# Ten warm-up matmuls instead of six, and the first MLP's residual keeps its mean until the last sums are added

## The chip, the core and the metric

The kernel runs on one core of a Trainium2 chip. Its time is in microseconds (us) of device time; several runs are taken and the median is compared. Beside the times there is the trace of one profiled execution, in which TensorE (PE, with its weight loads as PEld), VectorE (DVE), ScalarE (ACT), GpSimd (POOL) and the queue of SyncE (SP), which issues nearly all loads, are recorded instruction by instruction.

## The reference

A decoder trunk of two layers over 256 tokens of width 2048, in float32. The first layer mixes by a short gated convolution, the second by multi-head latent attention; behind each mixer stands an MLP of width 8192. Each of the four sub-layers ends in the same residual and normalisation:

```
h = layer_norm(ALPHA * h + mix, ln_g[layer, 0], ln_b[layer, 0])
h = layer_norm(ALPHA * h + sq_relu_mlp(h, mlp_w1[layer], mlp_w2[layer]), ln_g[layer, 1], ln_b[layer, 1])

def layer_norm(x, g, b):
    mu = mean(x, axis=-1)
    var = mean((x - mu) ** 2, axis=-1)
    return (x - mu) * rsqrt(var + LN_EPS) * g + b

def sq_relu_mlp(x, w1, w2):
    return square(relu(x @ w1)) @ w2
```

A layer norm gives the same result whatever is subtracted from all channels of a token beforehand. The kernel uses this to keep its sums of squares small.

## The kernel before

**Numbers and layout.** The float32 weights are split on the core into two parts, hi (a cast on ScalarE) and lo (a subtraction on VectorE), and TensorE multiplies hi and lo by the activations, which are split in the same way. The residual `xres` lies in SBUF as 16 chunks of 128 channels by 256 tokens: channels on the partitions, tokens along the row.

**The opening.** TensorE first runs `WARM` matmuls of a constant tile with itself into a PSUM tile `warm` that nobody reads. Then the first products (`ps_g`) are formed row by row of an array `opening` as its rows arrive: each row gives four matmuls with its hi part (`hifirst`) and four with its lo part (`lofirst`).

**The norms.** A `Norm` object with index 0 to 2 belongs to each of the first three normalisations; the last one is done elsewhere. `prepare(m)` works on chunk m of the residual: it multiplies by ALPHA and subtracts `mu0`. `mu0` is made at chunk 0 by one matmul with the tile `ones`, whose entries are 1/128: the mean over the first 128 channels of each token, copied by ScalarE from PSUM (`mu0p`) to SBUF (`mu`). `count` adds the chunk to the running sums S and Q, `wide` writes its weighted hi and lo parts `xd`, which the next layer's products read.

**The two MLPs.** `mlp(1, ...)` and `mlp(3, ...)` are one function. Its first part forms eight chunks of the hidden layer directly (`ps_w`). The middle part is planned: products of the first weight matrix (`ps_m`), and a Strassen form of part of the second (`sum1` to `sum7`, held in PSUM banks), are entered as operations of a list `Work`, with costs and dependences. A planner (`arrange`) simulates the engines, and `issue` then emits the instructions in the order it found. Ready operations of ScalarE and VectorE are taken by their due time; an operation that nobody waits for is due at the end and fills what is free. `work` receives the steps of the layer's input normalisation (`normals`), the loads and splits of weights, and, where the MLP is followed by another norm (`after`), the 15 `prepare` steps that are left behind chunk 0. `prepare(0)` is emitted ahead of the plan. The second MLP has no `after`, so its plan has no such steps.

**Behind the plan.** The sums of both column halves are combined on VectorE into eight blocks of 128 tokens by 512 channels: tokens on the partitions here. The rest of the second matrix is multiplied by `down` into PSUM tiles `ps_d`, and `put` adds each to its block. In the first MLP, `to_wide` transposes the blocks on TensorE (`turned`), adds them to `xres` with `add`, and counts and widens each chunk (`summed`). The next layer's first products start while the last blocks are still turned. PSUM tiles are given out in turn from two pools of four banks each.

**What sets the order.** Instructions of one engine run in the order in which they were emitted; engines wait for each other by semaphores. Nearly every instruction goes through one helper, so the profile puts nearly all of them on line L71, and they are told apart by the names of their tiles.

Of the kernel before, what the change touches and what calls it, by code (L numbers as in the profile page):

```python
# [10 lines left out]
F32 = mybir.dt.float32  # L11
F32R = mybir.dt.float32r
AF = mybir.ActivationFunctionType
ALU = mybir.AluOpType
AX = mybir.AxisListType

P = 128
W = 256 + 2
T = 256
D = 2048  # L20
NC = D // P
# [6 lines left out]
ALPHA = 4.0 ** 0.25  # L28
# [14 lines left out]
OPENS = T + OPEN * P  # L43
PLAIN = 2
GROUP = 3
WARM = 6
WO_G = 3

COL = 128
# [4 lines left out]
def trunk(ctx: ExitStack, tc: tile.TileContext, opening, xT, vecs, w_in, w_out, w_kv, w_q, w_uk, w_uv,  # L54
# [5 lines left out]
    class Engine:  # L60
# [3 lines left out]
        def __init__(self, engine):  # L64
            self.engine = engine
# [15 lines left out]
    scalar, vector, tensor, sync = (Engine(e) for e in (nc.scalar, nc.vector, nc.tensor, nc.sync))  # L81
    const = ctx.enter_context(tc.tile_pool(name="const", bufs=1))
    act = ctx.enter_context(tc.tile_pool(name="act", bufs=1))
# [3 lines left out]
    small = ctx.enter_context(tc.tile_pool(name="small", bufs=2))  # L87
# [49 lines left out]
    start = [0]  # L137
# [3 lines left out]
    class Banks:  # L141
# [15 lines left out]
        @classmethod  # L157
        def next(cls):
            cls.count += 1
            if cls.only is not None:  # L160
                return cls.only
            return cls.more if cls.more is not None and cls.count % 8 >= 4 else pmm
# [19 lines left out]
    def prepare(i):  # L182

        kind, *src = stream[i]
        if kind == "unit":
            raw = load_raw(i, src[0])
            hi, lo = ready[i] = parts(i)
            split(hi, lo, tiled(raw))
            yield
            return  # L190
        r1, r2 = (load_raw(f"{i}_{j}", v) for j, v in enumerate(src))

        def finished(r, name):
            w = parts(f"{i}_{name}")
            split(*w, tiled(r))
            return [[v.rearrange("p b c -> p (b c)")[:, o:o + BW] for v in w] for o in (0, BW)]

        out = {}
        out["11"], out["22"] = finished(r1, 1)
        yield  # L200
        out["21"], out["12"] = finished(r2, 2)
        ready[i] = out
        yield
# [24 lines left out]
    def psum(name):  # L228
        return Banks.next().tile([P, 512], F32, tag="mm", name=name)
# [38 lines left out]
    def mm_wide(wps, x, k0=0, k1=NC):  # L268

        for k in range(k0, k1):  # L270
            for w, ps in wps:
                hi, lo = (t[:, k % 8, :] for t in w[k // 8])
                tensor.matmul(ps[:, :W], hi, x[k][:, :W], start=k == 0, stop=False)
                tensor.matmul(ps[:, :W], lo, x[k][:, :W], start=False, stop=False)
                tensor.matmul(ps[:, :W], hi, x[k][:, W:], start=False, stop=k == NC - 1)

    def group_of(n):

        return [(take(), psum("ps_g")) for _ in range(n)]
# [26 lines left out]
    def down(x, put, n):  # L306

        ps = [psum("ps_d") for _ in range(2)]
        for j in range(len(x) // 2):
            w, = take(1)  # L310
            for kk in range(2):
                k = 2 * j + kk
                for t in range(2):
                    dot(ps[t], wide_rows(w, kk), held(x[k], t), k == 0, k == len(x) - 1)
        for t in range(2):
            put(n, t, ps[t])
# [30 lines left out]
    ones = const.tile([P, P], F32, name="ones")  # L347
    col = const.tile([P, COL], F32, name="col")
    vector.memset(ones, 1.0 / P)
    warm = psum("warm")  # L350
    for _ in range(WARM):
        tensor.matmul(warm[:, :P], ones, ones, start=True, stop=True)
# [23 lines left out]
    class Norm:  # L376
# [3 lines left out]
        def __init__(self, idx, scale):  # L380
            self.idx, self.scale = idx, scale
            self.S = act.tile([P, T], F32, tag="S", name=f"S{idx}")
            self.Q = act.tile([P, T], F32, tag="Q", name=f"Q{idx}")
            self.mu0 = act.tile([P, T], F32, tag="mu0", name=f"mu0{idx}")
            self.ws = None

        def prepare(self, m):

# [102 lines left out]
    def residual(ps, m):  # L491

        add(ps[:, T:], m)
        add(ps[:, :T], m)

    def add(ps, m):
        d = xres[:, m, :]
        vector.tensor_tensor(d, d, ps[:, :T], ALU.add)

    def summed(ln, pss, add, m0=0):  # L500

        for m, ps in enumerate(pss, m0):
            add(ps, m)
            ln.count(m)
            ln.wide(m)
# [4 lines left out]
    xres = act.tile([P, NC, T], F32, tag="xres", name="xres")  # L510
# [26 lines left out]
    ln = Norm(0, ALPHA)  # L537
    for m in range(NC):
# [3 lines left out]
        for what in "cub":  # L542
            ps = next(pss)
            f = cbuf[:, m % 2, "cub".index(what), :T]
# [226 lines left out]
    def mlp(idx, ln, after, blocks, fast):  # L771
# [14 lines left out]
        def pair():  # L786
            return fast.tile([P, 8 * P], F32, tag="sf", name="sf", bufs=2)
# [18 lines left out]
        for m in range(QC):  # L806
            if m < GROUP:
# [4 lines left out]
                ps = ws[m][1]  # L812
            else:
                ws = [(take(), psum("ps_w"))]
                mm_wide(ws, ln.xd)
                ps = ws[0][1]
            if m % 2 == 0:
                f = pair()
# [25 lines left out]

        layer, sums = idx // 2, Sums(idx)
        Banks.only = Banks.more
        if after is not None:
            after.prepare(0)
        work, freed, ring, place, entries, frees = Work(), {}, {}, {}, [], {}
        spans = {"A": lambda n: 0.82 * n + 110, "V": lambda n: n / 0.96 + 68}  # L850
        known = lambda deps: [d for d in deps if d is not None]
# [1 line left out]
        def add(engine, n, run, *deps, behind=(), early=0):  # L853
            return work.add(engine, spans[engine](n), run, known(deps), behind, early)
# [27 lines left out]
        normals = {}  # L882
        for k in todo:
# [1 line left out]
            x = add("V", 580, run, normals.get(k - 3))  # L885
            x = add("A", 880, run, x)
            normals[k] = add("V", 256, run, x)
        if after is not None:
            for k in range(1, NC):
                add("V", 256, lambda k=k: after.prepare(k), normals.get(k))  # L890

        fs, used, formed, emptied, halved = {}, {}, {}, [None, None], [None]

# [168 lines left out]
        def block(n, t):  # L1062
            return folded[n][t]

        def put(n, t, ps):
            vector.tensor_tensor(block(n, t), block(n, t), ps, ALU.add)

        h = [(one[:, k // 2, k % 2 * T:(k % 2 + 1) * T], two[:, k // 2, k % 2 * T:(k % 2 + 1) * T]) for k in range(QC)]
        blocks(block, put, h)

    def to_wide(block, put, h):

        def turned(n):
            for c in range(2):
                ps = psum("turned")
                for j in range(4):
                    src = block(n, j % 2)[:, (2 * c + j // 2) * P:(2 * c + j // 2 + 1) * P]
                    tensor.transpose(ps[:, j * P:(j + 1) * P], src, id_t)
                summed(ln, [ps[:, j * T:(j + 1) * T] for j in range(2)], add, 4 * n + 2 * c)

        ln.widen("b")
        for n in range(NB):
            down(h, put, n)
            if n:
                turned(n - 1)
        ln.ws = group_of(GROUP)
        mm_wide(ln.ws, ln.xd, 0, NC - 4)
        turned(NB - 1)
        mm_wide(ln.ws, ln.xd, NC - 4)

    before, ln = ln, Norm(1, ALPHA)


    with tc.tile_pool(name="fast1", bufs=1) as fast:
        mlp(1, before, ln, to_wide, fast)


    with tc.tile_pool(name="att", bufs=1) as ap:
# [63 lines left out]
        f = tmp.tile([P, T], F32, tag="fh", name="fpe", bufs=3)  # L1162
# [3 lines left out]
        for m in range(NK):  # L1166
            ps = next(pss)
# [23 lines left out]
        with tc.tile_pool(name="att2", bufs=2) as a2, \  # L1191
# [82 lines left out]
            after = Norm(2, ALPHA)  # L1274
# [73 lines left out]
    with tc.tile_pool(name="fast2", bufs=1) as fast:  # L1348
        mlp(3, after, None, to_out, fast)
# [88 lines left out]
```

## Time and profile before

| | |
|---|---|
| median of three runs | 2000.35 us (1997.7 to 2000.36) |
| the profiled execution | 2000.64 us |
| its span, first to last instruction | 1998.8 us |
| mean granted TensorE clock | 0.998 |
| busy: PE, DVE, ACT | 1981.9, 1763.3, 1392.6 us |
| HBM read | 383.35 MB, 193 GB/s over the span |

A row of the timeline is start, length, engine, line, operation, tiles (written <- read), shape and count, and in brackets the idle time of the engine before it and what ended it. Rows of equal instructions that follow each other are merged, with the length from the first start to the last end. Matmuls are pipelined: the length of one holds its way through the array, and the distance of two starts is what it takes of the engine. A float32 matmul that isn't split shows as two records. A row of the waits says who waited for whom, with the total in us, the number of times and the longest.

### The profile page before, as it was taken

How to read it: one execution, taken by the hardware profiler on the slowest of the kernel's cores; microseconds unless marked ns; L12 is line 12 of the kernel's file. 1: busy time of each engine (PE TensorE's matmuls, PEld its weight loads, DVE VectorE, ACT ScalarE, POOL GpSimd, SP SyncE). 2: the span in 40 equal slices, each digit the busy share in tenths (PEclk: the TensorE clock that was granted, in tenths of full speed). 3: DMA queues.
4: the chain of work that ended last, by engine and by line, in shares of the span. 5: the costliest groups of instructions: out<-in, count | busy, mean ns of one | idle time of the engine just before them, and what ended most of it. 6: DMA issues, size and time to landing. Idle time of an engine off the chain costs nothing.

```text
span 1998.8 us, 29668 instructions
## 1 busy us (share of the span) xinstructions
PE 1981.9 (99%) x11048; PEld 1733.6 (87%) x11048; DVE 1763.3 (88%) x2646; ACT 1392.6 (70%) x2070; POOL 2.3 (0%) x21
## 2 busy tenths in 40 slices
PE   9999999999999999999999999999999999999997
PEld 8888888988888888888889998898888888888886
DVE  7667667699999999999988888878999999999997
ACT  6444445577887888878856655557788888878871
POOL 0000000000000000000000000000000000000000
PEclk9999999999999999999999999999999999999999
DMA  9655555455666666666664543654666666666673
GB/s 337 230 189 187 189 190 188 155 164 185 208 200 208 203 200 201 203 208 205 214 218 156 165 126 115 209 161 156 196 204 198 204 202 208 205 204 203 199 240 119
DMA packets 107857, 387.39 MB, mean 194 GB/s; under 512 B 11968, under 2 KB 12736, under 8 KB 107712
## 3 DMA queue, kind: packets, MB, share of 16 engines
q1 hardware_dynamic: 107568, 385.36, 60.5%
q8 instruction: 86, 1.41, 0.3%
q14 instruction: 59, 0.48, 0.1%
q10 hardware_dynamic: 144, 0.13, 0.0%
HBM read 383.35 MB, written 2.10 MB: 193 GB/s over the span
## 4 chain that ended last, share of the span: by engine, by line
PE 85%; DVE 8%; ACT 3%; issue 2%; DMA 0%; DVEq 0%; ACTq 0%
PE ps_m L71 25%; PE sum L71 21%; PE ps_u L71 20%; PE ps_d L71 4%; PE ps_w L71 4%; PE ps_g L71 4%; DVE lo L71 4%; DVE w L71 2%; ACT hi L71 1%; PE ps_v L71 1%; PE ps_q L71 1%; PE S L71 1%; PE ps_k L71 1%; PE ps_wo L71 1%; ACT sums L71 1%
## 5 line engine op out<-in xcount | busy, mean ns | idle before, releaser
L71 DVE TENSOR_TENSOR lo<-w,hi 128x1024 fp32r<-128x1024 f32 x536 | 640.0, 1222 | 27.2 <-ACT hi L71 24.3
L71 ACT CAST hi<-w 128x1024 fp32r<-128x1024 f32 x536 | 530.8, 1055 | 141.7 <-DVE w L71 131.5
L71 ACT CAST hi<-raw 128x1024 fp32r<-128x1024 f32 x278 | 289.8, 1051 | 248.8 <-PE ps_u L71 154.9
L71 PE MATMUL ps_m<-xhl,hi 128*128 128x512 f32 x1792 | 446.3, 391 | 1.3 <-ACT hi L71 1.3
L71 DVE TENSOR_TENSOR lo<-raw,hi 128x1024 fp32r<-128x1024 f32 x278 | 334.0, 1222 | 112.3 <-ACT hi L71 39.6
L71 PEld LDWEIGHTS ps_m<-xhl,hi 128*128 128x128 f32 x1792 | 328.9, 188 | 65.6 <-ACT hi L71 1.9
L71 PE MATMUL sum<-hi,hc 128*128 128x512 f32 x736 | 277.9, 391 | 0.5 <-ACT sum L71 0.5
L71 PEld LDWEIGHTS ps_m<-xhl,lo 128*128 128x128 f32 x1792 | 244.3, 190 | 18.0 <-DVE lo L71 0.7
L71 PE MATMUL sum<-lo,hc 128*128 128x512 f32 x656 | 256.5, 391 | 0.0
L71 PE MATMUL ps_m<-xhl,lo 128*128 128x256 f32 x1792 | 250.0, 282 | 0.0
L71 PE MATMUL sum<-hi,ha 128*128 128x512 f32 x640 | 246.4, 389 | 0.0
L71 DVE TENSOR_TENSOR w<-w,w 128x512 f32<-128x512 f32 x312 | 214.5, 687 | 0.7
L71 PE MATMUL ps_u<-xhl_a,hi 128*128 128x512 f32 x704 | 168.1, 391 | 0.0
L71 PEld LDWEIGHTS sum<-hi,hc 128*128 128x128 f32 x736 | 138.6, 188 | 27.2 <-ACT sum L71 1.3
L71 PEld LDWEIGHTS ps_u<-xhl_a,hi 128*128 128x128 f32 x704 | 129.4, 188 | 25.1
L71 PEld LDWEIGHTS sum<-hi,ha 128*128 128x128 f32 x640 | 120.2, 188 | 25.9
L71 PEld LDWEIGHTS sum<-lo,hc 128*128 128x128 f32 x656 | 123.6, 188 | 21.5
L71 ACT COPY sums<-sum 128x512 f32<-128x512 f32 x194 | 109.7, 597 | 13.2 <-PE sum L71 12.6
L71 ACT COPY sum<-sums 128x512 f32<-128x512 f32 x174 | 104.3, 611 | 0.8
L71 ACT ACTIVATE sf<-sf 128x512 f32<-128x512 f32 x120 | 76.7, 639 | 26.9 <-DVE sf L71 25.8
L71 PE MATMUL ps_w<-xd,hi 128*128 128x258 f32 x512 | 94.3, 284 | 0.5 <-DVE xres L71 0.5
L71 PEld LDWEIGHTS ps_u<-xhl_a,lo 128*128 128x128 f32 x704 | 90.3, 191 | 3.4
(197 smaller groups left out, 2756.4 us busy)
## 6 DMA issues: line engine op xcount, KB each, us to landing
w<-in_w_dram SPq DMA_DIRECT2D x224, 512.0 KB, 3.9
w<-in_w2f_dram SPq DMA_DIRECT2D x208, 512.0 KB, 4.6
raw<-in_w_in_dram SPq DMA_DIRECT2D x88, 512.0 KB, 4.4
raw<-in_w_dram SPq DMA_DIRECT2D x64, 512.0 KB, 4.4
raw<-in_w_out_dram SPq DMA_DIRECT2D x32, 512.0 KB, 3.9
raw<-in_w_o_dram SPq DMA_DIRECT2D x32, 512.0 KB, 3.8
raw<-in_w2f_dram SPq DMA_DIRECT2D x16, 512.0 KB, 4.5
row<-in_opening_dram SPq DMA_DIRECT2D x15, 384.0 KB, 4.8
```

What stands on the lines that cost most here:

```text
L71: ins = op(*args, **named)
```

## The change

`WARM` goes from 6 to 10. For the first MLP's norm (index 1) the mean is no longer subtracted from the residual: neither `prepare(0)`, which stood ahead of the plan, nor the 15 planned `prepare` steps are issued. Behind the plan, `means` makes the mean over the first 128 channels as a column, one value per token, with the residual's chunk as stationary operand: two matmuls of one column into `mu0c`, and one small VectorE instruction that scales it to `off`. `put` now adds that column together with each `ps_d`, and `scaled` multiplies the residual by ALPHA while it adds the turned block. The other norms keep `prepare`.

```diff
-WARM = 6
+WARM = 10
...
-            self.mu0 = act.tile([P, T], F32, tag="mu0", name=f"mu0{idx}")
+            self.mu0 = act.tile([P, T], F32, tag="mu0", name=f"mu0{idx}") if idx != 1 else None
             self.ws = None
+
+        def means(self):
+
+            ps = psum("mu0c")
+            for t in range(2):
+                tensor.matmul(ps[:, t:t + 1], xres[:, 0, t * P:(t + 1) * P], ones[:, 0:1], start=True, stop=True)
+            self.off = small.tile([P, 2], F32, tag="off", name="off", bufs=1)
+            vector.tensor_scalar(self.off, ps[:, 0:2], -self.scale, None, ALU.mult)
...
+    def scaled(ps, m):
+        d = xres[:, m, :]
+        vector.scalar_tensor_tensor(d, d, ALPHA, ps, ALU.mult, ALU.add)
...
-        if after is not None:
-            after.prepare(0)
         work, freed, ring, place, entries, frees = Work(), {}, {}, {}, [], {}
...
-        if after is not None:
-            for k in range(1, NC):
-                add("V", 256, lambda k=k: after.prepare(k), normals.get(k))
...
         def put(n, t, ps):
-            vector.tensor_tensor(block(n, t), block(n, t), ps, ALU.add)
-
+            if after is None:
+                vector.tensor_tensor(block(n, t), block(n, t), ps, ALU.add)
+            else:
+                vector.scalar_tensor_tensor(block(n, t), ps, after.off[:, t:t + 1], block(n, t), ALU.add, ALU.add)
+
+        if after is not None:
+            after.means()
...
-                summed(ln, [ps[:, j * T:(j + 1) * T] for j in range(2)], add, 4 * n + 2 * c)
+                summed(ln, [ps[:, j * T:(j + 1) * T] for j in range(2)], scaled, 4 * n + 2 * c)
```

The order of the instructions moves at three places. On TensorE, where the first MLP's plan begins (`ps_w` are the last direct products, `sum` the first Strassen product), there stands before:

```order
L71 MATMUL ps_w<-xd_1_2667,lo_3857 128x258
L71 MATMUL ps_w<-xd_1_2667,hi_3856 128x258
L71 MATMUL mu0p<-xres,ones 128x256
L71 MATMUL sum_4183<-hi_1_3926,hc_3523 128x512
L71 MATMUL sum_4183<-lo_1_3927,hc_3523 128x512
```

and now:

```order
L71 MATMUL ps_w<-xd_1_2671,lo_3860 128x258
L71 MATMUL ps_w<-xd_1_2671,hi_3859 128x258
L71 MATMUL sum_4181<-hi_1_3929,hc_3526 128x512
L71 MATMUL sum_4181<-lo_1_3930,hc_3526 128x512
L71 MATMUL sum_4181<-hi_1_3929,hc_3526 128x512
```

The mean's matmul is gone; the products around it keep their order.

On VectorE, early in the same plan (`lo` a weight's low half, `nu` and `xhl` the normalisation of the input, `xres<-xres,mu` the prepare steps), there stands before:

```order
L71 TENSOR_TENSOR lo_0_4245<-w_4187,hi_0_4244 128x1024
L71 SCALAR_TENSOR_TENSOR xres<-xres,mu_3518 128x256 x3
L71 TENSOR_TENSOR xhl_3522<-xres,xhl_3522 128x256
L71 SCALAR_TENSOR_TENSOR xres<-xres,mu_3518 128x256
L71 TENSOR_TENSOR nu<-xres,ab_3734 128x256
L71 TENSOR_TENSOR nu<-nu,ab_3734 128x256
```

and now:

```order
L71 TENSOR_TENSOR lo_0_4243<-w_4185,hi_0_4242 128x1024
L71 TENSOR_TENSOR xhl_3525<-xres,xhl_3525 128x256
L71 TENSOR_TENSOR nu<-xres,ab_3737 128x256
L71 TENSOR_TENSOR nu<-nu,ab_3737 128x256
L71 TENSOR_TENSOR xhl_3525<-xres,xhl_3525 128x256
```

The prepare steps are gone and what stood behind them has moved up. Within the first twenty or so VectorE instructions, and the first fifty of ScalarE, counted from the first hidden chunks behind, other steps change places as well; from there to the end of the plan both engines have the order of the second MLP's plan, which is the same in both programs. TensorE's order within the plan and SyncE's order of loads are those of before.

On TensorE at the end of the plan (`ps_m` its last product, `ps_d` the first of `down`) there now stands:

```order
L71 MATMUL ps_m<-xhl_3525,hi_3_4355 128x512 x8
L71 MATMUL ps_m<-xhl_3525,lo_3_4356 128x256 x8
L71 MATMUL mu0c<-ones,xres 128x1 x2
L71 MATMUL ps_d<-hi_9002,hc_3526 128x512
L71 MATMUL ps_d<-lo_9003,hc_3526 128x512
```

Before, the first `ps_d` followed the last `ps_m` at once. On VectorE the small instruction behind `mu0c` stands between the last hidden chunk and the low halves of the down weights (`raw`):

```order
L71 TENSOR_TENSOR lo_9015<-raw_9012,hi_9014 128x1024
L71 TENSOR_TENSOR lo_9021<-raw_9018,hi_9020 128x1024
L71 TENSOR_TENSOR sf<-ps_m,t 128x256
L71 TENSOR_SCALAR off<-mu0c 128x2
L71 TENSOR_TENSOR xd_0_8995<-vec,xd_0_8995 128x16x2
L71 TENSOR_TENSOR lo_9027<-raw_9024,hi_9026 128x1024
L71 TENSOR_TENSOR lo_9033<-raw_9030,hi_9032 128x1024
```

All other rows there are those of before, one place later. With `mu0c` the turn of the PSUM banks moves by one from here: `mu0c` takes the bank that held `sum6`, the first `ps_d` that of `sum7`, the second that of `sum5`; before, the two `ps_d` had those of `sum6` and `sum7`.

## The prediction

> **What bounds the kernel now.** I read the page first (busy times, then the chain that ended last), then TensorE's own list of waits, then TensorE's timeline in the opening and at both ends of each MLP's plan.
>
> ```profile
> span 1998.8 us, 29668 instructions
> PE 1981.9 (99%) x11048; PEld 1733.6 (87%) x11048; DVE 1763.3 (88%) x2646; ACT 1392.6 (70%) x2070; POOL 2.3 (0%) x21
> PE 85%; DVE 8%; ACT 3%; issue 2%; DMA 0%; DVEq 0%; ACTq 0%
> ```
>
> TensorE is busy for 99% of the span and carries 85% of the chain. A busy share alone doesn't say that it never stands, so I read its waits over the whole span (total in us, times, longest):
>
> ```profile
> PE ps_m L71 <- ACT hi L71: 1.3, 3, 0.9
> PE ps_g L71 <- ACT hifirst L71: 1.2, 1, 1.2
> PE warm L71 <- DVE col L71: 1.0, 1, 1.0
> PE rstat L71 <- DVE csq L71: 0.8, 1, 0.8
> PE ps_w L71 <- DVE xres L71: 0.5, 1, 0.5
> PE sum L71 <- ACT sum L71: 0.5, 2, 0.3
> ```
>
> These six make 5.3 us of 1998.8; the rest of the list is shorter than 0.5 each. VectorE has 88% and yet TensorE hardly waits for it. So work that leaves VectorE or ScalarE is worth at most the part of these waits that it ends, while what leaves TensorE, or lets it run at full pace, counts in full.
>
> The profiled execution took 2000.64 us, 1.84 more than its span; the median of the three runs is 2000.35. I sum against 2000.64. A measurement of this kernel can tell about 0.2%, 4.0 us, from no change.
>
> **Part 1: four more warm-ups.** TensorE in the opening; start, length, tiles, count, idle time before:
>
> ```profile
> 1.05 2.93 PE L71 MATMUL warm<-ones 128*128 128x128 f32 x12 [1.05 <-DVE col L71]
> 5.22 2.04 PE L71 MATMUL ps_g<-xhl_a,hifirst 128*128 128x512 f32 x4 [1.25 <-ACT hifirst L71]
> 7.92 1.61 PE L71 MATMUL ps_g<-xhl_a,hifirst 128*128 128x512 f32 x4
> 9.84 1.09 PE L71 MATMUL ps_g<-xhl_a,hifirst 128*128 128x512 f32 x4
> 11.24 0.86 PE L71 MATMUL ps_g<-xhl_a,hifirst 128*128 128x512 f32 x3
> ```
>
> Each row of the opening array gives TensorE the same eight matmuls. The first takes 7.92 - 5.22 = 2.70 us, the second 1.92, the third 11.24 - 9.84 = 1.40. TensorE thus starts at about half pace and comes to its full one in the course of the second, some 3 to 4 us after 5.22. The six warm-ups (12 passes) with the idle 1.25 us behind them did not spare it this. The slow pace costs 1.30 + 0.52 = 1.82 us.
>
> Ten warm-ups are 20 passes. One takes about 0.23 us (2.93 less a tail of some 0.4, by 11 distances), so eight more take 1.8: the burst ends near 5.6, 0.4 us after the first real matmul could have started, and TensorE works unbroken from 1.05. The 3 to 4 us that it needed after 5.22 are then over at 4 to 5. If the pace doubles there, the last passes go faster, nothing is delayed and all of 1.82 is gained; if it doubles only with the end of the burst, 1.82 - 0.4 = 1.4. I take 1.4, the case in which the passes cost what the row shows. The other end is a loss of 0.4.
>
> The Trainium skill, "TensorE: Matmul & The Clock Gate", section "Part 1: The HAM clock gate", has a rule for this: the array's clock is halved until it was busy throughout one window of about 3.4 us, and these windows run on freely, whatever the kernel does. Half pace for 3 to 4 us agrees with it. By that rule alone the release could come up to two windows after 1.05, an estimate of 7.9, and the gain would lie anywhere between some 0.4 and 1.8.
>
> Is another engine then the opening's bound? Its last row of data, and TensorE where it uses it:
>
> ```profile
> 23.19 0.69 DVE L71 TENSOR_TENSOR lofirst<-row,hifirst 128x512 fp32r<-128x512 f32 x1
> 28.08 0.40 PE L71 MATMUL ps_g<-xhl_a,hifirst 128*128 128x512 f32 x1
> ```
>
> The data are split by 23.9, 4.2 us early, so a start 1.4 us sooner is covered.
>
> **Part 2: the mean leaves the head of the plan.** That place in the first MLP, and the same in the second, which has no mean there:
>
> ```profile
> 412.07 0.59 PE L71 MATMUL mu0p<-xres,ones 128*128 128x256 f32 x2
> 412.31 0.58 PE L71 MATMUL sum<-hi,hc 128*128 128x512 f32 x1
> 412.73 0.40 PE L71 MATMUL sum<-lo,hc 128*128 128x512 f32 x1
> 1357.15 0.39 PE L71 MATMUL sum<-hi,hc 128*128 128x512 f32 x1
> 1357.38 0.40 PE L71 MATMUL sum<-lo,hc 128*128 128x512 f32 x1
> ```
>
> From mu0p's start to the second sum matmul are 0.66 us, where one sum matmul takes 0.23 in the second MLP: 0.43 gained, of which 0.19 is the slow first sum behind it.
>
> **Part 3: 15 prepare steps leave VectorE's plan.** Their row for all three norms (count, total, mean in ns):
>
> ```profile
> L71 DVE SCALAR_TENSOR_TENSOR xres<-xres,mu 128x256 f32<-128x256 f32 x45 | 17.0, 424 | 0.0
> ```
>
> With chunk 0 they are 16 at 0.42 us here, some 7 us; ScalarE loses one copy. The new order from there on is the second MLP's, so the second MLP's trace is a preview. The last matmuls of both plans:
>
> ```profile
> 996.03 1.11 PE L71 MATMUL ps_m<-xhl,lo 128*128 128x256 f32 x8
> 1939.78 1.12 PE L71 MATMUL ps_m<-xhl,lo 128*128 128x256 f32 x8
> ```
>
> From the first sum to there the first MLP takes 996.03 - 412.31 = 583.72 us, the second 1939.78 - 1357.15 = 582.63. Of the 1.09 between them 0.19 are counted in part 2. The other 0.9 is a wait for hi. TensorE's waits within the first plan and, second row, within the second; then the load and the cast on which the first hangs, and the same pair in the second:
>
> ```profile
> PE ps_m L71 <- ACT hi L71: 1.1, 2, 0.9
> PE ps_m L71 <- ACT hi L71: 0.2, 1, 0.2
> 946.74 0.33 SPq L71 DMA_DIRECT2D w<-in_w_dram  x1
> 952.63 1.05 ACT L71 CAST hi<-w 128x1024 fp32r<-128x1024 f32 x1 [1.38 <-DMA w<-in_w_dram]
> 1891.53 0.33 SPq L71 DMA_DIRECT2D w<-in_w_dram  x1
> 1894.04 2.97 ACT L71 CAST hi<-w 128x1024 fp32r<-128x1024 f32 x3
> ```
>
> In the first MLP the cast began 5.9 us after its load was issued and had stood idle 1.38 for it; in the second it is the last of three casts without a gap. So the order leaves a margin, and one late load used it up. SyncE's order is unchanged and nothing in the change makes loads prompt: between 0 and 0.9 gained, I take half, 0.45. The 7 us of VectorE are otherwise worth nothing, for TensorE's matmuls hid them; were that cover gone, they would have shown as waits of TensorE for VectorE's lo, and the list has none.
>
> **Part 4: the mean behind the plan.** mu0c is two matmuls of one column on a full stationary operand, between ps_m and ps_d. Its nearest like is rstat, two of one column as well:
>
> ```profile
> 1082.15 0.60 PE L71 MATMUL rstat<-col,csq 128*128 128x1 f32 x4 [0.75 <-DVE csq L71]
> 1082.62 0.37 PE L71 MATMUL ps_w<-xd,hi 128*128 128x258 f32 x1
> ```
>
> 0.47 us to the next matmul, and that one is slow by 0.1 to 0.2, as the first sum behind mu0p was: 0.47 to 0.66, I take 0.6 lost. It adds waits: mu0c for the bank of sum6, the second ps_d for that of sum5. VectorE's adds that free them, TensorE's arrival, and what stands ahead of the new off:
>
> ```profile
> 987.69 0.70 DVE L71 TENSOR_TENSOR sums<-sums,sum 128x512 f32<-128x512 f32 x1
> 992.84 1.28 DVE L71 TENSOR_TENSOR sums<-sums,sum 128x512 f32<-128x512 f32 x2
> 996.99 0.40 PE L71 MATMUL ps_d<-hi,hc 128*128 128x512 f32 x1
> 997.84 0.42 DVE L71 TENSOR_TENSOR sf<-ps_m,t 128x256 f32<-128x256 f32 x1
> ```
>
> sum6 is free at 988.4, 8.6 us before TensorE comes; sum5 at 994.1, some 3.5 us before the second ps_d would start. VectorE reaches off at 998.3, when mu0c is through, so off waits for nothing; queued behind it are the gain columns and the lo halves for the following ps_d, each later by one instruction of two columns. Hidden, with the 3.5 us as cover.
>
> The last sums become three-operand instructions: put with a column as scalar, scaled with a constant. The plain adds, and the like of put; that of scaled is the prepare step's row, 0.424:
>
> ```profile
> L71 DVE TENSOR_TENSOR sums<-sums,ps_d 128x512 f32<-128x512 f32 x16 | 10.4, 682 | 8.3 <-PE ps_d L71 8.3
> L71 DVE SCALAR_TENSOR_TENSOR u<-sums,mv,gbt 128x512 f32<-128x512 f32 x8 | 5.9, 741 | 0.0
> L71 DVE TENSOR_TENSOR xres<-xres,turned 128x256 f32<-128x256 f32 x16 | 6.1, 416 | 0.9 <-PE turned L71 0.9
> ```
>
> Eight put at 0.06 more, 0.5 us, lie on VectorE under the next block's matmuls; without that cover they would cost 0.5. Of 16 scaled at 0.008 more, two lie in TensorE's wait ps_w <- DVE xres: 0.02 lost.
>
> **The sum.** -1.4 - 0.43 - 0.45 + 0.6 + 0.02 = -1.66 us; 2000.64 - 1.66 = 1998.98, so 1999.0.
>
> **Rivals.** *The pace comes no sooner.* The burst delays the first real matmul by 0.4 us and buys nothing: 2000.64 + 0.4 - 0.43 - 0.45 + 0.62 = 2000.8. For it speaks that six warm-ups bought nothing that the rows show; against it, that the idle 1.25 us go. Chance 0.21. The skill's freely running window, in the section named, would give this case where it stands badly against the kernel's start, and would make it change from run to run.
>
> *All of it at once.* The full 1.82, both waits of the first plan for hi (1.1), the mean: 2000.64 - 1.82 - 1.1 - 0.43 + 0.62 = 1997.9, about the fastest run shown before (1997.7). For it speaks the lighter VectorE, against it that the second MLP still waits. Chance 0.17. To be faster by over 0.2% the time must fall below 1996.35, which takes 1.5 us that I can't name; but the runs shown differ by 2.7, so I give that 0.07 of the 0.17.
>
> *TensorE stands at the borrowed banks* (slower). If VectorE is late at the end of the plan, mu0c and the second ps_d wait, and off holds the lo halves behind it. It decides where VectorE is more than 3.5 us later than here; each further us costs one. Above 2004.35 (slower by over 0.2%) it takes some 5.4 us more than that; at 9 us it would give 1999.0 + 5.5 = 2004.5. The late load of part 3 held a cast up by 1.4. Chance 0.04.
>
> **The numbers.** The forecast has 0.58; its own range is 1998.1 (1.82 and 0.9 instead of 1.4 and 0.45) to 1999.9 (a gain of 1.0 and no prompt load). The range that holds 8 in 10 takes in the first rival and the second with a little of the runs' spread: 1996.8 to 2001.1. Faster by over 0.2%: 0.09, the 0.07 and a little of the forecast; slower: 0.06, the third rival and 0.02 for what I overlook; within 0.2%: 0.85.
>
> **What would show it.** Right: the first two rows of ps_g less than 1.6 us apart, the first near 5.5; the first sum at once behind ps_w; 582.6 us from it to the last ps_m; ps_d 0.5 to 0.7 us later than at once. Wrong: first rows still 2.7 and 1.9 us apart; a gap ahead of mu0c or the second ps_d; more than 1 us of waits for hi or lo in the first plan.

## The result, and the profile after

The changed kernel takes 2002.46 us (median of 22 runs, 2001.75 to 2003.03), the kernel before, run beside it, 1999.72 (median of 22, 1997.69 to 2001.81). The ratio is 1.0013, with a 95% interval of 1.0007 to 1.0018. So it is slower, by some 2.7 us, less than the 0.2% that the prediction set as its bound; the forecast was 1.7 us faster, and its range ended at 2001.1. The profiled execution took 2003.01 us, 2.37 more than the one of before.

Span, busy times and shares of the chain in the page of the changed kernel:

```profile
span 2001.2 us, 29669 instructions
PE 1986.2 (99%) x11058; PEld 1733.7 (87%) x11058; DVE 1758.8 (88%) x2630; ACT 1392.3 (70%) x2069; POOL 2.3 (0%) x21
PE 94%; DVE 3%; issue 1%; ACT 1%; DMA 1%; SPq 0%; DVEq 0%; ACTq 0%
```

TensorE's share of the chain has grown from 85% to 94%, its busy time by 4.3 us, while its longest wait for `hi` is gone (TensorE's waits, after):

```profile
PE ps_g L71 <- ACT hifirst L71: 0.8, 1, 0.8
...
PE ps_m L71 <- ACT hi L71: 0.3, 2, 0.2
```

So the engine doesn't stand more; it works longer. TensorE's timeline of the changed kernel, at the places that the prediction named, says where:

```profile
411.19 0.39 PE L71 MATMUL sum<-hi,hc 128*128 128x512 f32 x1
411.43 0.40 PE L71 MATMUL sum<-lo,hc 128*128 128x512 f32 x1
...
996.33 1.12 PE L71 MATMUL ps_m<-xhl,lo 128*128 128x256 f32 x8
997.28 0.50 PE L71 MATMUL mu0c<-ones,xres 128*128 128x1 f32 x4
997.65 0.47 PE L71 MATMUL ps_d<-hi,hc 128*128 128x512 f32 x1
997.96 0.39 PE L71 MATMUL ps_d<-lo,hc 128*128 128x512 f32 x1
...
1357.55 0.39 PE L71 MATMUL sum<-hi,hc 128*128 128x512 f32 x1
...
1942.15 1.11 PE L71 MATMUL ps_m<-xhl,lo 128*128 128x256 f32 x8
```

At the first sum it is 1.12 us ahead of before (412.31), as was hoped. Then the first plan takes 996.33 - 411.19 = 585.14 us instead of 583.72, and the lead is gone at the first `ps_d` (0.66 behind). The second plan, in which the change touches no instruction, takes 1942.15 - 1357.55 = 584.60 instead of 582.63. That is 1.97 us, with no wait to show for it. The grouped rows name the matmuls; of before, then of after (count, total us, mean ns):

```profile
L71 PE MATMUL sum<-t,hc 128*128 128x512 f32 x216 | 65.8, 389 | 0.0
L71 PE MATMUL sum<-t,ha 128*128 128x512 f32 x96 | 37.3, 389 | 0.0
```

```profile
L71 PE MATMUL sum<-t,hc 128*128 128x512 f32 x216 | 67.3, 396 | 0.0
L71 PE MATMUL sum<-t,ha 128*128 128x512 f32 x96 | 38.1, 397 | 0.0
```

`t` is the tile `t4`, hi and lo of the one Strassen factor that has a place of its own. Matmul by matmul, the order in the second plan is the same, and the two traces differ in two places: the three that read `t4` take 0.86 us more in sum, the five behind each three 1.24, and all the rest 0.13 less. One such group in the second plan, before and then after:

```profile
1424.55 0.84 PE L71 MATMUL sum<-t,hc 128*128 128x512 f32 x3
1425.23 0.39 PE L71 MATMUL sum<-hi,ha 128*128 128x512 f32 x1
...
1425.91 1.98 PE L71 MATMUL ps_m<-xhl,hi 128*128 128x512 f32 x8
1427.72 0.52 PE L71 MATMUL ps_m<-xhl,lo 128*128 128x256 f32 x3
```

```profile
1425.08 0.86 PE L71 MATMUL sum<-t,hc 128*128 128x512 f32 x3
1425.79 0.39 PE L71 MATMUL sum<-hi,ha 128*128 128x512 f32 x1
...
1426.48 1.99 PE L71 MATMUL ps_m<-xhl,hi 128*128 128x512 f32 x8
1428.30 0.28 PE L71 MATMUL ps_m<-xhl,lo 128*128 128x256 f32 x1
```

From the first `t` matmul to the last `ps_m` row these fourteen take 3.17 us before and 3.22 after, 0.05 more. The 216 + 96 matmuls on `t4` are 104 visits of three in the two plans; 1.97 us in one plan is 0.04 for each of its 52.

What has changed for `t4`? The order shows nothing, and neither does the diff, until one looks where the program, as built from each kernel, puts its tiles. The new tile `off` has 8 bytes per partition and takes a slot of 32 in the pool `small`. The pools behind it move on by 32 bytes: `t4` from byte 224896 of each partition to 224928. Before, `hi`, `lo`, `xhl`, `hc` and `t4` all begin at 128 past a multiple of 512; now `t4` alone of TensorE's operands in the plan is out of step with them. That gives the theory, **addresses**: the 32 bytes cost about 4 us in the two plans, and the change itself gains what was forecast. Its rival, **edits**: more warm-ups or the lighter order slow TensorE later on, wherever the tiles lie.

### The profile page after: what moved, and what is told of

Read it like the earlier page. It is cut to its first block, busy times and chain, and to the rows that moved or that the text cites. A ratio compares the mean times of both kernels' runs of the same rounds, so it can differ in the third digit from the quotient of the medians.

```text
span 2001.2 us, 29669 instructions
## 1 busy us (share of the span) xinstructions
PE 1986.2 (99%) x11058; PEld 1733.7 (87%) x11058; DVE 1758.8 (88%) x2630; ACT 1392.3 (70%) x2069; POOL 2.3 (0%) x21
## 4 chain that ended last, share of the span: by engine, by line
PE 94%; DVE 3%; issue 1%; ACT 1%; DMA 1%; SPq 0%; DVEq 0%; ACTq 0%
PE ps_m L71 29%; PE sum L71 25%; PE ps_u L71 20%; PE ps_d L71 4%; PE ps_w L71 4%; PE ps_g L71 4%; PE ps_q L71 1%; PE ps_v L71 1%; DVE lo L71 1%; PE S L71 1%; PE ps_k L71 1%; PE ps_wo L71 1%; PE po L71 1%; DVE w L71 1%; PE ps_p L71 1%
```

## The experiments

In the expectations a plan's length counts to the last single `ps_m`, 0.83 us behind the row used here. All medians are beside runs of the kernel before on the same chip, whose medians were 2000.13 to 2000.41.

**`off` back out of the pool.** The changed kernel with

```diff
-            self.off = small.tile([P, 2], F32, tag="off", name="off", bufs=1)
+            self.off = col[:, 8:10]
```

> The changed kernel, but off takes two unused columns of the tile col and no place of its own, so all tiles lie where they lay before. Addresses (the 32 bytes by which the new tile off moves t4 slow every matmul that reads t4): about 4.4 us less than the changed kernel, 1998 to 1998.5, below the kernel before; from the first sum to the last ps_m 584.6 or less in the first MLP and 583.5 in the second, as before. Edits (more warm-ups or the new order slow TensorE): about 2002.5 as the changed kernel, with 586.0 and 585.4 between these points.

Measured: 1998.30 us (1997.93 to 1998.9), 0.9991 of before (0.9983 to 1.0000), 4.2 below the changed kernel with no overlap of the runs. Its `t` row, and the ends of its plans:

```profile
L71 PE MATMUL sum<-t,hc 128*128 128x512 f32 x216 | 65.8, 389 | 0.0
```

```profile
410.38 0.39 PE L71 MATMUL sum<-hi,hc 128*128 128x512 f32 x1
...
993.42 1.12 PE L71 MATMUL ps_m<-xhl,lo 128*128 128x256 f32 x8
...
1354.61 0.39 PE L71 MATMUL sum<-hi,hc 128*128 128x512 f32 x1
...
1937.20 1.11 PE L71 MATMUL ps_m<-xhl,lo 128*128 128x256 f32 x8
```

583.04 and 582.59 us: the extra time is gone from both plans, with every edit of the change still there.

**The 32 bytes alone.** The kernel before with

```diff
+        if after is not None:
+            vector.memset(small.tile([P, 2], F32, tag="off", name="off", bufs=1), 0.0)
```

> The kernel before, with a tile of two columns in the pool in which off would lie and one small memset of it behind the first plan; nothing else of the change. Addresses: 4.4 us slower than before, about 2004, with 586 and 585.4 us from the first sum to the last ps_m in the two MLPs and the extra time at the three matmuls that read t4 and the few behind them. Edits: as before, 1999.7, but for some 0.1 us of the memset.

Measured: 2003.66 us (2000.92 to 2004.48), 1.0016 of before (1.0007 to 1.0025). Its second plan, and its `t` row:

```profile
1357.85 0.39 PE L71 MATMUL sum<-hi,hc 128*128 128x512 f32 x1
...
1942.43 1.12 PE L71 MATMUL ps_m<-xhl,lo 128*128 128x256 f32 x8
```

```profile
L71 PE MATMUL sum<-t,hc 128*128 128x512 f32 x216 | 67.3, 396 | 0.0
```

584.58 us, and 396 ns as in the changed kernel. With both runs the edits fall as a cause of this extra time, and the shift of 32 bytes is shown: it makes the change's extra time where none of the edits is, and leaves with it where all of them are.

**Warm-ups alone.** The kernel before with `WARM = 10`.

> The kernel before with ten warm-ups, nothing else; all tiles where they lay. Prediction, part 1: 1.4 us less than before (1998.3). By the trace of the changed kernel: 0.9 less (1998.8), since the third row of the opening array comes late, with a smaller spread of the runs. If more warm-ups slow TensorE later on: over 2001, with 585.4 us from the second MLP's first sum to its last ps_m.

Measured: 1998.32 us (1997.61 to 1999.05), 0.9990 (0.9982 to 0.9999). The medians differ by 1.84, with an interval of 0.2 to 3.6 us, which holds the 1.4 of the prediction as well as a full 1.82. In the trace, the fourth row of the opening array and the first sum of the plan stand at:

```profile
9.79 1.09 PE L71 MATMUL ps_g<-xhl_a,hifirst 128*128 128x512 f32 x4
...
410.83 0.58 PE L71 MATMUL sum<-hi,hc 128*128 128x512 f32 x1
```

Before, these stood at 11.24 and 412.31: in this profile the opening gained 1.45 and kept it. With `off` in `col` the fourth row stands at 9.52, a gain of 1.72, and in the changed kernel at 10.36, a gain of 0.88. A further 0.9 us came in the first plan, where the profile with warm-ups alone has less of the waits for `hi`. Its second plan takes 582.58 us, as before, so more warm-ups slow nothing later on. The opening of the changed kernel, and of the one with `off` in `col`:

```profile
1.05 4.27 PE L71 MATMUL warm<-ones 128*128 128x128 f32 x20 [1.05 <-DVE col L71]
5.07 1.18 PE L71 MATMUL ps_g<-xhl_a,hifirst 128*128 128x512 f32 x4
...
6.56 1.08 PE L71 MATMUL ps_g<-xhl_a,hifirst 128*128 128x512 f32 x4
...
8.88 1.17 PE L71 MATMUL ps_g<-xhl_a,hifirst 128*128 128x512 f32 x4 [0.77 <-ACT hifirst L71]
```

```profile
5.23 1.17 PE L71 MATMUL ps_g<-xhl_a,hifirst 128*128 128x512 f32 x4
...
6.71 1.09 PE L71 MATMUL ps_g<-xhl_a,hifirst 128*128 128x512 f32 x4
...
8.11 1.09 PE L71 MATMUL ps_g<-xhl_a,hifirst 128*128 128x512 f32 x4
```

In both the first row of the array takes 1.5 us instead of 2.70. In the first profile the third row of data came late, and TensorE, now early enough to meet it, waited 0.77; of the eight profiles with ten warm-ups this is the only one. With ten warm-ups the runs of one kernel lie 1.0 to 1.4 us apart, with six 1.8 to 4.1.

**The mean alone.** The changed kernel with `off` in `col` and `WARM = 6`.

> The changed kernel with six warm-ups and off in two columns of col: the mean's part of the change alone, with all tiles where they lay. Prediction, parts 2 to 4: 0.43 + 0.45 - 0.6 - 0.02 = 0.26 less than before. By the traces of the changed kernel and of the one with off in col, where mu0c took 0.37 and the wait for the late load did not come: 0.2 to 1.0 less than before.

Measured: 1999.93 us, 0.9999 (0.9990 to 1.0008): a gain of 0.4 by the medians, within what was expected, but these runs can't tell it from none.

**Which places, and how far.** The changed kernel with `t4` alone put back onto a multiple of 64 bytes (224960):

```diff
-                    box["f"] = fast.tile([P, 2, BW], F32R, tag="t4", name="t4", bufs=1)
+                    t4 = fast.tile([P, 2 * BW + 8], F32R, tag="t4", name="t4", bufs=1)
+                    box["f"] = t4[:, 8:8 + 2 * BW].rearrange("p (a c) -> p a c", a=2)
```

> The changed kernel with off in its own place, but t4 begins 32 bytes into a tile that is 32 bytes longer, so t4 alone begins at a multiple of 64 bytes again (224960) and the other tiles that off moved stay moved. If t4's place alone counts: as with off in col, about 1998 to 1998.5. If the other moved tiles count (sf, or those of attention): part or all of the 4.4 us stays, 2000 to 2002.5. Edits: 2002.5.

Measured: 2004.30 us (2003.89 to 2004.98), a miss: worse than 32 bytes, though aligned to 64. So it isn't alignment to 64. The next five, all made from the kernel before, ask two things: by how many bytes `t4` must move until the cost is gone again (the grain), and whether its place counts by itself or against the other operands. With the pool's extra tile 64 bytes long instead of 32:

> The kernel before with a tile of 64 bytes where off would lie, so sf and t4 lie 64 bytes further (t4 at 224960, where it lay in the run with t4 alone moved). Grain of 64 bytes: as before, 583.4 us from the second MLP's first sum to its last ps_m. Grain of 128 bytes: as in the run with t4 moved alone, 586.6 there and some 6 us in all, about 2005 to 2006. If it was the longer t4 tile or sf and t4 lying apart that cost the 586.6: below 585.4.

With it 128 bytes long:

> The kernel before with a tile of 128 bytes there, so that sf and t4 lie 128 bytes further (t4 at 225024, a multiple of 128). Grain of 128 bytes: no change but for the memset, 583.4 in the second MLP, about 1999.7. Any move of t4 costs: 585 or more there, 2003 or more. A grain above 128 bytes: likewise.

With it 256 bytes long:

> The kernel before with a tile of 256 bytes where off would lie: sf and t4 lie 256 bytes further, so t4 begins at 384 past a multiple of 512 while hi, lo, xhl and hc all begin at 128 past one. If the distance counts modulo 256: no change, 583.4 from the second MLP's first sum to its last ps_m, 1999.7 to 2000.2 in all. If modulo 512: 585 or more there, 2002.8 or more in all.

With `t4` alone 16 bytes on, by the edit above with 4 elements in place of 8:

> The kernel before, with t4 alone starting 16 bytes into a longer tile (224912); all else where it lay. t4's place alone counts with any offset: 585 or more from the second MLP's first sum to its last ps_m, 4 us or more in all. A grain of 16 bytes or less: 583.4, as before. If the cost comes from sf and the tiles of attention, not t4: 583.4 too.

And with everything moved together:

```diff
-    vec = const.tile([P, 2 * P], F32, name="vec")[:, :C_END]
+    vec = const.tile([P, 2 * P + 16], F32, name="vec")[:, :C_END]
```

> The kernel before with the first constant tile 64 bytes longer, so that nearly all tiles, t4 and the other operands of TensorE, lie 64 bytes further and keep their distances. If the place by itself counts (grain of 128 bytes): every matmul that reads 128x512 is some 8 ns slower, that is 20 us and more over the kernel, 2020 or above. If only t4's place against the other operands counts: as before, 1999.7 and 583.4.

Measured, with the second plan from its first sum to its last `ps_m` row, and what that is more than before:

| `t4` moved by, against the others | median us | ratio (95%) | second plan | more |
|---|---|---|---|---|
| 16 bytes | 2005.37 | 1.0026 (1.0015 to 1.0037) | 585.19 | 2.56 |
| 32 (only the tile added) | 2003.66 | 1.0016 (1.0007 to 1.0025) | 584.58 | 1.95 |
| 64 | 2005.98 | 1.0032 (1.0020 to 1.0045) | 585.77 | 3.14 |
| 128 | 2002.84 | 1.0014 (1.0005 to 1.0023) | 584.33 | 1.70 |
| 256 | 1999.52 | 0.9997 (0.9988 to 1.0006) | 582.60 | 0.0 |
| 0 (all tiles by 64) | 2000.10 | 1.0003 (0.9994 to 1.0012) | 582.59 | 0.0 |

Every distance tried that is no multiple of 256 costs; 256 doesn't, and moving all tiles together doesn't. So a place has no price by itself: what costs is the distance between operands, and of the distances tried only 256 bytes, beside none, is free. A grain of 128 bytes, one of the cases written down, is refuted by the fourth row. `sf` moved with `t4` in four of the rows; in the first it stayed and the cost came all the same. And with `t4` at 64 and `sf` at 32, the run before these, the second plan took 585.75, as in the row for 64. So `t4`'s place against the other operands is what counts. With 16 bytes the three matmuls that read it lose only 0.15 us in the second plan; nearly all of the 2.56 lies in the ten behind them.

**Against which operand?** Half the tiles moved, `raws`, `hi`, `lo` and `t4` by 64 bytes against `xhl`, `hc` and `ha`. The kernel before with

```diff
-            ab = act.tile([P, 2 * T], F32, tag="ab", name=f"ab{self.idx}")
+            ab = act.tile([P, 2 * T + 16], F32, tag="ab", name=f"ab{self.idx}")[:, :2 * T]
```

> The kernel before with the tile ab 64 bytes longer, so that every tile behind it (hi, lo, t4) lies 64 bytes further and those ahead of it (xhl, hc, ha) do not. In the plan each matmul then has its moving and its stationary operand 64 bytes out of step, while moving operands that follow each other stay in step except where sum and ps_m follow each other. If moving against stationary counts: all the plan's matmuls of 512 columns are slower, by some 4 to 8 ns each, 10 to 20 us in each plan, over 2020 in all. If a moving operand against the one ahead of it counts: about 25 to 50 ns at each of some 50 to 100 changes from sum to ps_m, 2 to 4 us in each plan, 2004 to 2008. If nothing of this counts but t4 alone: 2000.

Measured: 1999.33 us, 0.9997 (0.9988 to 1.0005). By the time this is the third case, but by the trace it is not as before: the second plan takes 1938.91 - 1355.71 = 583.20 us, 0.57 more, and the pitch of its matmuls has moved. A chunk of `ps_m` in the second plan, of before and then of this kernel:

```profile
1415.56 1.98 PE L71 MATMUL ps_m<-xhl,hi 128*128 128x512 f32 x8
1417.37 1.12 PE L71 MATMUL ps_m<-xhl,lo 128*128 128x256 f32 x8
1418.33 2.00 PE L71 MATMUL ps_m<-xhl,hi 128*128 128x512 f32 x8
1420.17 1.11 PE L71 MATMUL ps_m<-xhl,lo 128*128 128x256 f32 x8
1421.12 0.40 PE L71 MATMUL sum<-hi,hc 128*128 128x512 f32 x1
```

```profile
1414.34 2.03 PE L71 MATMUL ps_m<-xhl,hi 128*128 128x512 f32 x8
1416.21 1.07 PE L71 MATMUL ps_m<-xhl,lo 128*128 128x256 f32 x8
1417.12 2.02 PE L71 MATMUL ps_m<-xhl,hi 128*128 128x512 f32 x8
1418.98 1.08 PE L71 MATMUL ps_m<-xhl,lo 128*128 128x256 f32 x8
1419.89 0.39 PE L71 MATMUL sum<-hi,hc 128*128 128x512 f32 x1
```

Eight matmuls of 512 columns went from 1.81 to 1.87 us in the first piece, eight of 256 from 0.96 to 0.91. The chunk as a whole takes 5.55 us, before 5.56. That suggested a layout in which only `lo`, which is the stationary operand of the 256-column ones, is out of step. The changed kernel with a gap between the rings of `hi` and `lo` (and a longer `off`, so that `t4` stays in step):

```diff
+        if i == "first0":
+            whl.tile([P, 16], F32, tag="gap", name="gap", bufs=1)
...
-            self.off = small.tile([P, 2], F32, tag="off", name="off", bufs=1)
+            self.off = small.tile([P, 48], F32, tag="off", name="off", bufs=1)[:, :2]
```

> The changed kernel with 64 bytes between the ring of hi and the ring of lo, and off 192 bytes long, so that lo alone lies 64 bytes out of step and sf and t4 lie 256 bytes on, in step. In the plan's ps_m, hi is the stationary operand of matmuls of 512 columns and lo that of matmuls of 256. Moving against stationary: the ps_m from lo go from 120 to 113.5 ns as in the run with half the tiles moved, 1712 x 6 ns = some 10 us less over both plans, those from hi stay at 227; the sums whose moving operand is lo lose 2 to 5 ns each, 688 x 3.5 = 2.4 us; in all about 1990 to 1993, faster than both kernels. A moving operand against the one ahead of it: ps_m from lo stay at 120, the sums lose, 2000 to 2006.

With a gap of 128 and of 192 bytes (and `off` of 128 and of 64):

> The same with 128 bytes between the rings of hi and lo (off 128 bytes long, t4 in step). Moving against stationary, and the distance of 128 free or better for 256 columns: 113 to 120 ns for a ps_m from lo, 1990 to 1998. If t4's 32, 64 and 128 bytes cost in sum what they cost there for any moving operand out of step: the sums from lo 1 to 5 ns slower each, and ps_m from lo as before: 2000 to 2003.

> The same with 192 bytes between the rings, that is lo 64 bytes short of being in step where the first of these is 64 past it. If the sign of the distance doesn't matter: as with 64. If it does: ps_m from lo nearer to 120 ns, 1996 to 2002.

Measured: 2007.42 us (ratio 1.0036, 1.0024 to 1.0049), 2012.39 (1.0062, 1.0050 to 1.0075) and 2003.24 (1.0016, 1.0007 to 1.0025): slower, all three. Against the kernel with `off` in `col`, 1998.30, they lose 9.1, 14.1 and 4.9 us. The chunk with 64 bytes, as above:

```profile
1417.58 2.00 PE L71 MATMUL ps_m<-xhl,hi 128*128 128x512 f32 x8
1419.42 1.11 PE L71 MATMUL ps_m<-xhl,lo 128*128 128x256 f32 x8
1420.36 2.00 PE L71 MATMUL ps_m<-xhl,hi 128*128 128x512 f32 x8
1422.20 1.11 PE L71 MATMUL ps_m<-xhl,lo 128*128 128x256 f32 x8
1423.14 0.39 PE L71 MATMUL sum<-hi,hc 128*128 128x512 f32 x1
...
1428.03 0.39 PE L71 MATMUL ps_m<-xhl,hi 128*128 128x512 f32 x1
```

The chunk takes 5.56 us as before: the two eights of `lo` save 0.03 together (0.94 and 0.94), and the first eight of `hi` loses as much (1.84). The 21 sums behind it, in which moving operands in and out of step follow each other, take 1428.03 - 1423.14 = 4.89 us, where before has 1425.91 - 1421.12 = 4.79. These 0.10, at 52 such groups, are of the size of the whole loss in the second plan: 1945.80 - 1358.41 = 587.39 us, 4.76 more than before. So the stationary operand's place does change the pitch a little, but a loss is seen where moving operands that follow each other lie out of step. I expected the first to be some 10 us faster and was wrong. Nor is the rule complete. In the run with half the tiles moved, `sum` and `ps_m` follow each other out of step and the plan lost only 0.57; 128 bytes cost the least for `t4` and the most here; and 64 bytes short of being in step cost about half of 64 past it, so the sign matters. What TensorE compares inside, and why the same `lo` at the same distance gave 0.91 for eight in one kernel and 0.94 in the other, stays open.

**The best of these.** `off` in `col`, ten warm-ups, and the longer `ab`:

> The changed kernel with off in two columns of col and with the tile ab 64 bytes longer, so that all tiles behind ab lie 64 bytes further: the whole change, with the layout that had the smallest time of those tried with six warm-ups. If layout and warm-ups add up: 1999.33 from the run with half the tiles moved, less 1.84 that ten warm-ups brought, is 1997.5. If the layout's 1.0 was chance: 1998.3, as with off in col alone.

Measured: 1997.81 us (1997.18 to 1998.44), 0.9987 of before (0.9978 to 0.9996), the fastest of all, though with ranges that overlap those of 1998.30. The traces speak against chance, but it is not the plans that gain: the second takes 1936.40 - 1353.21 = 583.19 us, 0.60 more than with `off` in `col` alone. What gains lies outside them: from the first plan's last `ps_m` row to the second plan's first sum it is 1353.21 - 992.83 = 360.38 us instead of 1354.61 - 993.42 = 361.19. The same layout with six warm-ups has 360.14 there, where before has 361.12. Which matmuls gain there stays open.

## Why the prediction was wrong

**The step that failed** is part 3's claim that the second MLP's trace is a preview, 582.6 us from the first sum to the last `ps_m`, and with it a term that the sum put silently at nothing: that the matmuls which aren't edited keep their pitch. The prediction looked at what the new tile `off` makes engines wait for, and not at where the tile makes the others lie. The second plan took 584.60 us where the run with `off` in `col` has 582.59, the first 585.14 where that has 583.04: 2.0 + 2.1 us. The medians, 2002.46 - 1998.30, give 4.2 for the place of `t4` (4.6, if each is taken against the runs of before beside it). Take that away, and the whole change comes to 1.9 us less than before (interval 0.0 to 3.4), where I forecast 1.7: the terms were right together as far as these runs can tell, and one was missing. None of my rivals had it. The slower one, TensorE at the borrowed banks, did not come: there is no gap ahead of `mu0c`, and the fourth `ps_d` matmul, the first into the second tile, starts one pitch behind the third:

```profile
998.19 0.40 PE L71 MATMUL ps_d<-hi,ha 128*128 128x512 f32 x1
998.43 0.40 PE L71 MATMUL ps_d<-hi,hc 128*128 128x512 f32 x1
```

Of the three signs that were to show the prediction wrong none came: they stood for its own rivals, and could not show a term that was missing. Among the signs of being right, the 582.6 us failed, with 585.14.

**Part 1, the warm-ups: right.** The full pace came sooner in every profile with ten: the array's first eight matmuls take 1.47 to 2.30 us and the second eight 1.4 (without the one wait for data), where all nine profiles with six have 2.70 and then 1.57 to 2.56. The rival that the pace comes no sooner is refuted by the run with warm-ups alone. The first `ps_g` came 0.2 to 0.4 us ahead of the 5.5 that was forecast, because the burst was shorter than worked out. I had looked only at the last row of data for the cover; the third is the one that can be late, and took 0.77 back in the profiled run. The moment of the full pace still wanders: with `lo` 128 bytes away, ten warm-ups left the `hifirst` half of the array's first row at half pace, and its eight matmuls took 7.64 - 5.34 = 2.30 us. The Trainium skill, "TensorE: Matmul & The Clock Gate", section "Part 1: The HAM clock gate", says that the window runs on freely, so that the release moves from run to run; the 1.47 to 2.30 us agree with it. Whether it is also why the runs lie closer together with ten warm-ups is not shown.

**Part 2, the mean at the head: right.** The first two sums are 411.43 - 411.19 = 0.24 us apart at once behind `ps_w`, so 0.42 of the 0.43 came.

**Part 3, the late load: 0.45 forecast, 0.9 in the profile, and not by the lighter order.** `ps_m` stands 0.25 us in the first plan of the changed kernel, where before has 1.14. But the long wait for `hi` is also absent with warm-ups alone, where the prepare steps are still in the plan (582.86 us for the first plan there). So taking the half between two ends was a hedge, and the gain proves nothing for the removed steps. Whether it is chance is open: in all eight profiles with ten warm-ups `ps_m` stands 0.1 to 0.3 us in the first plan, in the nine with six 0.2 to 1.4, and in seven of these over 0.4. Why an earlier start should matter there is not shown.

**Part 4, the mean behind the plan: 0.6 forecast, 0.45 measured.** `mu0c` takes 997.65 - 997.28 = 0.37 us, and the first `ps_d` behind it is slow by 0.08. The three-operand sums cost nothing that shows in TensorE's waits. One slip in the sums of the forecast: the upper end of its own range, 2000.64 - 1.0 - 0.43 + 0.62, is 1999.8 and not 1999.9; nothing hangs on it.

## What to carry to other kernels

A small new tile can move every pool that is allocated behind it. When a change adds or drops one, compare the addresses of the matmuls' operands too, modulo 256 bytes as far as it was tried here, or put the new data into a place that exists. When a region that the change doesn't touch gets slower with no wait to show for it, compare the pitch of the same matmuls in the two traces before looking for a cause in the order. And an experiment that undoes only the side effect, here one line, separates it from the edit better than any that undoes the edit.

## What the hardware showed that I had not expected

Moving one operand of TensorE by 16 to 128 bytes against the others slows the three 512-column matmuls that read it and, in sum more, the five to ten behind them, 1.70 to 3.14 us in a plan, 0.03 to 0.06 on the mean for each of its 52 visits; a move by 256 bytes is free, and so is moving all together by 64. Half the tiles 64 bytes away make eight 512-column matmuls slower (1.81 to 1.87) and eight 256-column ones faster (0.96 to 0.91). The granted clock was 0.998 in all these profiles but two, with 0.999, so the clock doesn't tell the slow ones from the fast.
